# The value columns of a gated block: two column groups by a seven-product scheme, and twelve gate dot products moved to the last stage

## The chip, the cores and the metric

The kernel runs on one core of one Trainium2 chip. TensorE (PE) multiplies matrices, VectorE (DVE) and ScalarE (ACT) work on elements, GpSimd (POOL) and SyncE (SP) here mostly issue transfers, which all share the core's 16 DMA engines. The metric is the device time of one execution in microseconds; lower is better.

## The reference, cut to what matters

One layer on 512 tokens of width 2048, all in float32:

```python
shift, scale, gate = split(silu(c) @ W_ada + b_ada, 3)
h = rmsnorm(x) * (1 + scale) + shift
q_lat, kv_lat, k_rope, z_mla, u, v, z_sgu, g_mla, g_sgu = split(h @ W_in)
A = attention(q_lat, kv_lat, k_rope) * silu(z_mla)           # 16 heads, causal
B = u * (tril(W_s) @ rmsnorm(v) + b_s) * silu(z_sgu)         # 16 column groups, chunks of 128 tokens
x = x + gate * ((sigmoid(g_mla) * A + sigmoid(g_sgu) * B) @ W_out)
return rmsnorm(x)
```

The change touches how the 2048 columns of v are computed (`h @ W_in[:, v]`, a product of 512 x 2048 by 2048 x 2048) and when the 2048 values of `gate` are (each a dot product of silu(c) with one column of W_ada).

## The kernel before, in words

**Precision.** Each float32 operand is split in a high part (`hi`, a cast to the fast float32 format by ScalarE) and a low part (`lo = x - hi`, by VectorE). A product is three matmuls: hi hi, lo hi, hi lo (`mm3`). A tile of 128 x 1024 weights is a granule; class `Stream` (`ws`) loads granules in order on SP's queue into three buffers (`wraw0..2`) and splits them into two places of parts (`w0`, `w1`), one granule ahead of the matmuls.

**Stages.** (1) Two streams `w1`, `w2` give the latents; meanwhile VectorE takes the dot products of W_ada for scale and shift (`ada_dot`, one 128 x 2048 tile each, 16 values per 128 columns and part) and the input is scaled in place (`fix_to`) into `hh[j]` (high) and `hl[j]` (low), 16 chunks of 128 inputs by 512 tokens. (2) The columns of v with those of k_rope, in five column groups of widths `VW`, tokens on the partitions: for each of 8 granules, 2 chunks and 4 blocks of 128 tokens one `mm3` into four banks (line 518). At the end of a group `evac_v` takes the sum of squares and copies the bank out, and the copy is stored to `v_d`. Beside them VectorE runs the 16 dots for `gate` (`gate_step`), scales the latents (`lat_scale`), and makes sums and differences of quarters of the input (`make_sums`, `split_sum`, tiles s1, s2, s3, s4). Then one plain column group (z of head 14) runs, 4 slots from -4 to -1. (3) The main stage: columns of z, g, u, s, t in pairs. Each pair takes seven products of 1024 inputs by 256 tokens by 128 columns instead of eight (Strassen's scheme, Winograd's form): the right sides are the quarters of the input and s1 to s4, the left ones quarters of the weights and their sums, made by VectorE (`add`) or by accumulating transfers of GpSimd. A slot is one product, 24 matmuls of 256 tokens (lines 1267 to 1269).

**The order around the change** is written out beforehand. `on(s, phase, f)` puts work at slot s in a phase (FIRST, EVAC, GATE, SPLIT, BACK, then after the matmuls MISC, LOAD); `place(s, us, f)` seeks the first slot from s on in which VectorE's planned time stays under 2.75 us (`spend` books it). A product's weights are split two slots ahead, into three places w0, w2, w1. Every engine works its queue in order. Functions in `early` run at a step of stage 2; those in `pend` are taken one at a time as granules are fetched; `stores` issues a store one step after its copy. (4) Attention, head by head. (5) The output product: four column groups of 512 with 8 granules each (`out_granule`), `residual` after each, which multiplies with `grow`, the gate broadcast to all partitions, read from `gate_row` in memory. `gate_to_row` (line 877) transposes the gate on TensorE and writes that row in slot 10 of the main stage. The granules of the fourth group are split early into tiles of their own (`last_tiles`).

Of the kernel before, what the change touches and what calls it, by code (L numbers as in the profile page):

```python
# [11 lines left out]
F32 = mybir.dt.float32  # L12
# [8 lines left out]
P = 128  # L21
D = 2048
S = 512
# [13 lines left out]
VW = (512, 512, 384, 384, 320)  # L37
# [3 lines left out]
DOTS = (3, 3, 4, 5, 5, 6, 7, 8, 9, 9, 10, 11, 11, 12, 12, 13, 13, 14, 14, 15, 16, 16, 16, 16)  # L41
FIXED = (0, 0, 0, 0, 2, 2, 2, 2, 2, 4, 4, 4, 6, 6, 8, 8, 10, 10, 12, 12, 14, 16, 16, 16)
# [73 lines left out]
def trunk_layer(ctx, tc, xT, xn, c, vecs, pos, wada, w1, w2, wv, wv3, wv4, wh, wh15, wq, wqr, wk, wvv, wo, wsT, bsp, gfin, out,  # L116
# [91 lines left out]
    gate_row = scratch("gate_row", [KC, P])  # L208
    v_d = scratch("v_d", [NB, P, D])
# [42 lines left out]
    def last_tiles():  # L252
        k = len(dlast)
        dlast.append((nt(dp[0].p, [P, GW], F32R, f"dh{k}"), nt(dp[0].p, [P, GW], F32R, f"dl{k}")))
        return dlast[-1]

    go = {}
# [238 lines left out]
    for n, i in enumerate((8, 0, 9, 12, 1, 10, 11, 2, 7, 3, 4, 5, 6)):  # L496
        early.setdefault(8 + n, []).append(lambda i=i: lat_scale(i))
# [4 lines left out]
    for j in range(8):  # L502
        at_ = 12 + 5 * j // 2
        early.setdefault(at_, []).append(lambda j=j, at_=at_: sums_begin(j, at_))
        early.setdefault(32 + j, []).append(lambda j=j: split_sum("s4", j, s4f[j]))
    for cg, w in enumerate(VW):
        psv = [bank()[:, :w] for _ in range(4)]
        for i in range(8):
            g = cg * 8 + i
            wH, wL = get(gv[g], ahead=1)  # L510
            if g < 8:
                fix_to(FIXED[KC + g], lambda: dot_to(DOTS[KC + g]))
            for k in range(2):
                j = 2 * i + k
                sl = slice(k * w, (k + 1) * w)
                for n in range(NB):
                    tk = slice(n * P, (n + 1) * P)
                    mm3(psv[n], hh[j][:, tk], hl[j][:, tk], wH[:, sl], wL[:, sl], j == 0, j == KC - 1)
            for j in gate_step.get(g, ()):
                ada_dot(2 * KC + j)  # L520
            if g == 31:
                ada.close()
                c1[0] = Scope("c1", side=RIGHT)
                for n in ("s4h", "s4l"):
                    sums[n] = nt(c1[0].p, [P, 8, 256], F32R, n)
            for f in early.pop(g, ()):
                f()
            stores()
        if cg == 0:
# [4 lines left out]
            tb = Scope("tB")  # L534

        def evac_v(n, cg, ps):
            m = VW[cg] // P
            w, c0 = m * P, sum(VW[:cg])
            junk = nt(tb.p, [P, S], F32, f"t{n % 2}") if cg == 0 else nt(latp.p, [P, S], F32, f"lat{10 + n % 2}")
            ACT.activation(junk[:, :w], ps[:, :w], AF.Square, accum_out=ssv[:, n, cg:cg + 1])  # L540
            t = nt(tb.p, [P, S], F32, "sig", bufs=2)
            ACT.copy(t[:, :VW[cg]], ps[:, :VW[cg]])
            store(v_d[n][:, c0:c0 + w], t[:, :w])
            if cg == 4:
                store(kr_d[n], t[:, w:VW[cg]])

        for n in range(NB):
            pend.append(lambda n=n, cg=cg, ps=psv[n]: evac_v(n, cg, ps))
# [6 lines left out]
    pend.append(v_norm)  # L555
# [1106 lines left out]
```

## Time and profile before

| | |
|---|---|
| median of 3 runs | 1610.45 us (1609.62 to 1610.47) |
| profiled execution | 1609.98 us, its span 1608.3 us |
| PE / DVE / ACT busy | 99% / 72% / 47% of the span |
| two 512-wide groups of v | 154.31 to 241.35 us |
| two 384-wide groups, one of 320 | 241.35 to 309.17 to 337.32 us |
| plain column group | 337.32 to 348.23 us |
| main stage | from 348.23 us |
| output product | from about 1422 us, between the last head's work |

The page gives busy time by engine, forty slices of the span with granted clock and DMA load, the DMA queues, the chain of work that ended last, the costliest groups of instructions and the DMA issues. In a row of a group stand line, engine, operation, tiles out<-in, shape, count, busy time, mean ns of one, and the idle time before it with what ended it. Matmuls are pipelined, so a matmul's own duration is longer than its distance from the next.

### The profile page before, as it was taken

Reading aid. Unit: us, or ns where it says so; the run is one execution under the profiler, and the core shown is the slowest. Engines: PE = TensorE matmul, PEld = TensorE weight load, DVE = VectorE, ACT = ScalarE, POOL = GpSimd, SP = SyncE. Lnnn points to the kernel's source line nnn. Section 1 sums busy time; section 2 is a strip of 40 time slices with the busy share of each in tenths; the row PEclk is TensorE's granted clock in tenths of the full one; section 3 lists DMA queues with packets and bytes.
Section 4 is the critical chain, followed back from the end, with each engine's and each line's share of the span. In section 5 each row is a group of like instructions: output and inputs, shape, how many; then the busy total and the mean of one; then the engine's idle time right before and its main releaser. Section 6 shows DMA issues by size and latency. Waiting matters only on the chain.

```text
span 1608.3 us, 26988 instructions
## 1 busy us (share of the span) xinstructions
PE 1594.2 (99%) x10760; PEld 1488.5 (93%) x10760; DVE 1165.3 (72%) x1719; ACT 755.5 (47%) x1259; POOL 105.4 (7%) x128
## 2 busy tenths in 40 slices
PE   9999999999999999999999999999999999999997
PEld 8888889999999999999999999999988889888886
DVE  8989679658777777777677777666777888763453
ACT  4443334355545454454465554554655554542322
POOL 0000000001111111111111111112000000000000
PEclk9999999999999999999999999999999999999999
DMA  9988489568899897898887998887422233336422
GB/s 379 354 296 317 171 280 324 170 193 202 219 253 252 226 252 214 233 258 212 231 253 203 250 268 207 238 193 181 162 87 88 82 105 89 90 109 227 136 87 105
DMA packets 122766, 329.64 MB, mean 205 GB/s; under 512 B 14072, under 2 KB 35600, under 8 KB 115856
## 3 DMA queue, kind: packets, MB, share of 16 engines
q1 hardware_dynamic: 104768, 269.72, 48.0%
q0 software_dynamic: 17872, 58.20, 20.8%
q8 instruction: 84, 1.38, 0.3%
q14 instruction: 42, 0.34, 0.1%
HBM read 303.95 MB, written 23.93 MB: 204 GB/s over the span
## 4 chain that ended last, share of the span: by engine, by line
PE 90%; DVE 4%; DMA 2%; ACT 1%; issue 1%; SPq 0%; DVEq 0%; ACTq 0%
PE ps L1267 15%; PE ps L1269 15%; PE ps L1268 15%; PE ps L136 14%; PE ps L137 14%; PE ps L135 14%; PE ps L1429 1%; DVE wada L126 1%; PE ps L1392 1%; PE ps L1393 1%; DVE t L123 1%; DMA wraw<-in_w 1%; DMA lat<-v_d 1%; DVE lat L123 1%; DMA rope_d<-half 0%
## 5 line engine op out<-in xcount | busy, mean ns | idle before, releaser
L106 DVE TENSOR_TENSOR w0l<-wraw,w0h 128x1024 fp32r<-128x1024 f32 (+3 forms) x74 | 78.8, 1066 | 58.8 <-ACT w0h L105 58.5
L105 ACT CAST w1h<-wraw 128x1024 fp32r<-128x1024 f32 (+3 forms) x74 | 63.9, 863 | 118.8 <-PE ps L137 57.7
L1267 PE MATMUL ps<-hh,w0h 128*128 128x256 f32 x416 | 118.5, 285 | 0.9 <-DVE lat L123 0.9
L105 ACT CAST w0h<-wraw 128x1024 fp32r<-128x1024 f32 (+3 forms) x74 | 68.9, 931 | 106.6 <-PE ps L137 66.5
L1269 PE MATMUL ps<-hh,w0l 128*128 128x256 f32 x416 | 117.7, 283 | 0.0
L1268 PE MATMUL ps<-hl,w0h 128*128 128x256 f32 x416 | 117.7, 283 | 0.0
L106 DVE TENSOR_TENSOR w1l<-wraw,w1h 128x1024 fp32r<-128x1024 f32 (+3 forms) x74 | 73.1, 988 | 59.6 <-ACT w1h L105 58.6
L1267 PE MATMUL ps<-hh,w2h 128*128 128x256 f32 x400 | 113.5, 284 | 0.0
L1267 PE MATMUL ps<-hh,w1h 128*128 128x256 f32 x400 | 113.4, 283 | 0.0
L1268 PE MATMUL ps<-hl,w1h 128*128 128x256 f32 x400 | 113.2, 283 | 0.0
L1269 PE MATMUL ps<-hh,w2l 128*128 128x256 f32 x400 | 113.2, 283 | 0.0
L1268 PE MATMUL ps<-hl,w2h 128*128 128x256 f32 x400 | 113.2, 283 | 0.0
L1269 PE MATMUL ps<-hh,w1l 128*128 128x256 f32 x400 | 113.2, 283 | 0.0
L126 DVE SCALAR_TENSOR_TENSOR wada<-wada,cact 128x2048 f32<-128x2048 f32 x47 | 107.1, 2280 | 0.0
L123 DVE TENSOR_TENSOR w2l<-raw,w2h 128x1024 fp32r<-128x1024 f32 x56 | 68.5, 1224 | 39.0 <-ACT w2h L649 38.9
L136 PE MATMUL ps<-w0l,hh 128*128 128x256 f32 (+3 forms) x288 | 92.7, 322 | 0.1
L135 PE MATMUL ps<-w0h,hh 128*128 128x256 f32 (+3 forms) x288 | 92.7, 322 | 0.0
L137 PE MATMUL ps<-w0h,hl 128*128 128x256 f32 (+3 forms) x288 | 92.4, 321 | 0.0
L135 PE MATMUL ps<-hh,w1h 128*128 128x512 f32 x226 | 89.7, 397 | 0.0
L136 PE MATMUL ps<-hl,w1h 128*128 128x512 f32 x226 | 88.3, 391 | 0.8 <-DVE hl L126 0.8
L137 PE MATMUL ps<-hh,w1l 128*128 128x512 f32 x226 | 88.1, 390 | 0.0
L629 POOL DMA_DIRECT2D wraw<-in_wh x67 | 59.2, 939 | 439.8 <-DVE w0l L123 211.7
(350 smaller groups left out, 5400.5 us busy)
## 6 DMA issues: line engine op xcount, KB each, us to landing
raw<-in_wh SPq DMA_DIRECT2D x105, 512.0 KB, 6.9
wada<-in_wada SPq DMA_DIRECT2D x47, 1024.0 KB, 7.4
wraw<-in_wh POOLq DMA_DIRECT2D x67, 512.0 KB, 6.9
wraw<-in_wh SPq DMA_DIRECT2D x45, 512.0 KB, 7.8
raw<-in_wh POOLq DMA_DIRECT2D x42, 512.0 KB, 7.8
wraw<-in_wo SPq DMA_DIRECT2D x32, 512.0 KB, 3.7
half<-in_w SPq DMA_DIRECT2D x35, 256.0 KB, 5.4
wraw<-in_w SPq DMA_DIRECT2D x16, 512.0 KB, 8.9
```

Source lines behind the costliest of these rows:

```text
L105: self.nc.scalar.copy(hi[:, :n], raw[:, :n])
L106: self.nc.vector.tensor_tensor(out=lo[:, :n], in0=raw[:, :n], in1=hi[:, :n].bitcast(F32), op=ALU.subtract)
L123: DVE.tensor_tensor(out=out, in0=in0, in1=in1, op=op)
L126: DVE.scalar_tensor_tensor(out=out, in0=in0, scalar=scalar, in1=in1, op0=op0, op1=op1, **kw)
L135: PE.matmul(ps, ah, bh, start=start, stop=False)
L136: PE.matmul(ps, ah, bl, start=False, stop=False)
L137: PE.matmul(ps, al, bh, start=False, stop=stop)
L629: q_.dma_start(t, wh[h, n, q // 10 - 1], **eng)
L1267: PE.matmul(ps, wH[:, sl], xh, start=st, stop=False, skip_group_check=True)
L1268: PE.matmul(ps, wH[:, sl], xl, start=False, stop=False, skip_group_check=True)
L1269: PE.matmul(ps, wL[:, sl], xh, start=False, stop=sp, skip_group_check=True)
L1392: PE.matmul(ps, q2[:, q], krh[:, :n], start=False, stop=False)
```

## The change: what it does

- Columns 0 to 1023 of v, two groups of 512 before, are computed together by the seven-product scheme: quarters of the input are 1024 inputs by 256 tokens, quarters of the weights 1024 inputs by 512 columns. `V7` lists 28 steps (product, granule of two chunks), placed at slots -28 to -1; a step has 2 chunks x 2 token blocks x 3 matmuls with the tokens as the stationary operand and 512 columns moving. The sums of the weights are made by VectorE (`v_sum`, `v_t3`) and, for product 4, by accumulating transfers of GpSimd. The results are combined from banks y, z, w by `v_copy`, `v_c12`, `v_c22`, `v_c11`, `v_c21`.
- The three narrower groups come first (26 steps with the plain column group's two granules among them), then the seven products, then the main stage. The plain columns go to memory (`z_d`) and are loaded back.
- Of the 16 dots for the gate four stay in stage 2 (`NG`); twelve (`chunk_load`, `chunk_sum`) go to the output product, one per granule. For them silu(c) is stored (`cact_d`) and broadcast back. The gate is written to `gate_row` in four parts straight from its column form (`gate_out`), and read in four parts (`grow_load`); the transpose goes. The tiles for the fourth group lie in two scopes of their own.
- The main stage's first loads are placed at slots -7 to -2; the sums s1 to s4 are made some steps earlier; v's norm (`v_norm`) moves to slot 1.

```diff
-VW = (512, 512, 384, 384, 320)
+VW = (384, 384, 320)
+VC = (1024, 1408, 1792)
+
+V7 = [(p, i) for i in range(4) for p in (1, 6)] + [(p, i) for i in range(4) for p in (2, 7)]
+V7 += [(3, i) for i in range(4)] + [(p, i) for i in range(4) for p in (5, 4)]
+NG = 4
 WARM = (32, 48)
 CR = 8
 
-DOTS = (3, 3, 4, 5, 5, 6, 7, 8, 9, 9, 10, 11, 11, 12, 12, 13, 13, 14, 14, 15, 16, 16, 16, 16)
-FIXED = (0, 0, 0, 0, 2, 2, 2, 2, 2, 4, 4, 4, 6, 6, 8, 8, 10, 10, 12, 12, 14, 16, 16, 16)
+DOTS = (3, 3, 4, 5, 5, 6, 7, 8, 9, 9, 10, 11, 11, 12, 12, 13, 13, 14, 14, 15, 16, 16, 16, 16, 16)
+FIXED = (0, 0, 0, 0, 2, 2, 2, 2, 2, 4, 4, 4, 6, 6, 8, 8, 10, 10, 12, 12, 14, 14, 16, 16, 16)
...
-    gv = [ws.add(src[i], 2 * w) for w, src in zip(VW, (wv[0], wv[1], wv3[0], wv3[1], wv4)) for i in range(8)]
     gq, gr, gk, gvv = {}, {}, {}, {}
     c1 = [None]
-    gz = [ws.add(wh[H - 2, 0, half], GW) for half in range(2)]
-    ws.limit = gz[1]
+
+    def third_place():
+        return [nt(c1[0].p, [P, GW], F32R, tag) for tag in ("w2h", "w2l")]
+
+
+    steps = [("z", 0)] + [(0, i) for i in range(8)] + [("z", 1)] + [(cg, i) for cg in (1, 2) for i in range(8)]
+    gb = []
+    for cg, i in steps:
+        if cg == "z":
+            gb.append(ws.add(wh[H - 2, 0, i], GW))
+        else:
+            last = (cg, i) == (2, 7)
+            gb.append(ws.add((wv3[0], wv3[1], wv4)[cg][i], 2 * VW[cg], to=third_place if last else None))
+    ws.limit = gb[-1]
...
-    gate_step = {}
-    for j in range(KC):
-        st = 8 + (3 * j) // 2
-        gate_step.setdefault(st, []).append(j)
-        load_before(gv[0] + st + 1 if st < 31 else gv[0] + 31, ada_load, 2 * KC + j)
+    for j in range(NG):
+        load_before(gb[8 + j], ada_load, 2 * KC + j)
+    load_before(g2[0], lambda: DMA.dma_start(cact_d, cact[0:1]))
...
+    kept_at = [(lambda: c1[0].p, "raw7")] + [(lambda: wp, f"wraw{i}") for i in (1, 2, 0)]
+    kept, passing, vparts = {}, {}, {}
+
+    def v_kept(i):
+        p, tag = kept_at[i]
+        kept[i] = nt(p(), [P, GW], F32, tag)
+        DMA.dma_start(kept[i], wv[1][i])
+
+    def v_pass(what, i):
+
+        n = len(passing)
+        t = passing[what, i] = nt(c1[0].p, [P, GW], F32, ("raw6", "raw4", "raw5")[n % 3])
+        g, half = {"11": (0, 0), "11b": (0, 0), "21": (0, 4), "22": (1, 4)}[what]
+        DMA.dma_start(t, wv[g][half + i])
+
+    def v_sum(what, i):
+        tt(kept[i], kept[i], passing[what, i], ALU.add)
+
+    def v_t3(i):
+        t = passing["11b", i]
+        tt(t, kept[i], t, ALU.subtract)
+
+    def v_split(g):
+        p, i = V7[g]
+        t = kept[i] if p in (6, 2, 4) else passing[{1: "11", 7: "22", 3: "11b", 5: "21"}[p], i]
+        pl, tag = [(wp, "w1"), (wp, "w0"), (c1[0].p, "w2")][g % 3]
+        vparts[g] = hi, lo = nt(pl, [P, GW], F32R, tag + "h"), nt(pl, [P, GW], F32R, tag + "l")
+        hilo(hi, lo, t)
+
+    for at_, f, *a in ((20, v_pass, "11", 0), (21, v_kept, 0), (22, v_pass, "11", 1), (23, v_kept, 1), (24, v_kept, 2),
+                       (24, v_pass, "11", 2), (24, v_split, 0), (25, v_kept, 3), (25, v_sum, "11", 0), (25, v_split, 1),
+                       (25, v_pass, "11", 3)):
+        early.setdefault(at_, []).append(lambda f=f, a=a: f(*a))
+
+    plain = bank()
+    v_banks = [(4, 5, 6, 7), (0, 1, 2, 4), (5, 6, 7, 3)]
+    ring_ = [6, 7, 0, 1, 2]
+    assert (n_bank[0] - 1) % 8 == 3
+    psv = {}
...
+    def gate_sum(a, b):
+
+        cols = slice(a, b)
+        tt(gate[:, cols], dots[:, 2 * KC + a:2 * KC + b], vec[:, C_BADA + 2 * KC + a:C_BADA + 2 * KC + b], ALU.add)
+
+    def gate_out(a, b):
+        DMA.dma_start(gate_row[a:b].rearrange("j p -> p j"), gate[:, a:b])
 
     def v_norm():
-        tt(gate, dots[:, 2 * KC:], vec[:, C_BADA + 2 * KC:C_BADA + 3 * KC], ALU.add)
+        gate_sum(0, NG)
...
+    V = -len(V7)
+    for g in range(len(V7)):
+        spend(V + g - 2, 1.22)
+    v_events = [(V - 2 + 2 * i, GATE, v_sum, "11", i) for i in range(1, 4)]
+    v_events += [(V + 5 + 2 * i, GATE, v_sum, "22", i) for i in range(4)]
+    v_events += [(V + s, GATE, v_t3, i) for i, s in enumerate((13, 14, 16, 17))]
+    for s, *_ in v_events:
+        spend(s, 1.22)
+    v_events += [(V + g - 2, SPLIT, v_split, g) for g in range(2, len(V7))]
+    for what, slots in (("22", (1, 3, 5, 8)), ("11b", (10, 12, 14, 15)), ("21", (16, 17, 18, 19))):
+        v_events += [(V + s, LOAD, v_pass, what, i) for i, s in enumerate(slots)]
+    v_events += [(V + 15 + i, LOAD, lambda i: nc.gpsimd.dma_start(kept[i], wv[0][4 + i], accum_op=ALU.add), i)
+                 for i in range(4)]
+    for s, ph, f, *a in v_events:
+        on(s, ph, f, *a)
     for j in range(8):
-        place(-2 + j // 4, 0.42, lambda j=j: hilo(hh[j][:, right], hl[j][:, right], s3f[j]))
+        assert place(V + 1, 0.42, lambda j=j: split_sum("s4", j, s4f[j])) < V + 8 + j // 2
+    for j in range(8):
+        assert place(V + 6, 0.42, lambda j=j: hilo(hh[j][:, right], hl[j][:, right], s3f[j])) < V + 15 + j // 2
+    v7 = {}
+
+    def v_copy(name, ps, tags):
+        for t in range(2):
+            v7[name, t] = slot(tags[t]) if tags[t][:3] == "lat" else nt(tb.p, [P, S], F32, tags[t])
+            ACT.copy(v7[name, t], v7[ps][t])
+
+    def v_done(s, n, part, c0, t, src=None):
+
+        ACT.activation(slot("lat12") if src is None else t, src or t, AF.Square, accum_out=ssv[:, n, part:part + 1])
+        if src is not None:
+            ACT.copy(t, src)
+        on(s + 1, LOAD, lambda: DMA.dma_start(v_d[n][:, c0:c0 + 512], t))
+
+    def v_c12(s):
+        for t in range(2):
+            o = v7["u2", t]
+            tt(o, v7["z"][t], o, ALU.subtract)
+            v_done(s, t, 3, 512, o)
+
+    def v_c22(s):
+        for t in range(2):
+            o = v7["z6", t]
+            tt(o, o, v7["y"][t], ALU.subtract)
+            v_done(s, 2 + t, 3, 512, o)
+
+    def v_c11(s):
+        for t in range(2):
+            o = v7["p1", t]
+            tt(o, v7["w"][t], o, ALU.add)
+            v_done(s, t, 4, 0, o)
+
+    def v_c21(s):
+        for t in range(2):
+            v_done(s, 2 + t, 4, 0, slot(("lat7", "lat9")[t]), v7["y"][t])
+
+    on(V + 7, EVAC, v_copy, "p1", "y", ("lat11", "lat4"))
+    on(V + 8, EVAC, v_copy, "z6", "z", ("lat5", "lat6"))
+    on(V + 15, EVAC, v_copy, "u2", "y", ("t0", "t1"))
+    on(V + 18, EVAC, v_c12, V + 18)
+    on(V + 20, EVAC, v_c22, V + 20)
+    on(V + 27, EVAC, v_c11, V + 27)
+    on(0, EVAC, v_c21, 0)
+    on(1, EVAC, v_norm)
+    on(2, LOAD, gate_out, 0, NG)
+    for s in (18, 20, 27):
+        spend(V + s, 1.38)
...
-    def gate_to_row():
-        pg = bank()
-        PE.transpose(pg[:KC, :P], gate, ident)
-        row = sig()[:KC, :P]
-        DVE.tensor_copy(row, pg[:KC, :P])
-        DMA.dma_start(gate_row, row)
-
-    on(10, MISC, gate_to_row)
...
+    for g, (p, i) in enumerate(V7):
+        s = done[0] = V + g
+        for f in pend[:1]:
             f()
-        del pend[:2]
+        del pend[:1]
+        for f in early.pop(len(steps) + g, ()):
+            f()
         if s == -1:
-            while pend:
-                pend.pop(0)()
+            assert not pend and not early
             tb.close()
             mis = Scope("more")
             sg[0] = Scope("sgu")
-        run(s, FIRST, EVAC, GATE)
-        if s == -4:
-            plain = bank_at(plain_bank)
-        for k in range(4):
-            j = (s + 4) * 4 + k
-            sl = slice(j % 8 * P, (j % 8 + 1) * P)
-            mm3(plain, wH[:, sl], wL[:, sl], hh[j], hl[j], j == 0, j == KC - 1)
-        run(s, SPLIT, BACK, MISC, LOAD)
+        run(s, FIRST, EVAC, GATE, SPLIT, BACK)
+        if i == 0 and p in (1, 5, 6):
+            which, banks = {1: ("y", (2, 4)), 6: ("z", (0, 1)), 5: ("w", (5, 6))}[p]
+            v7[which] = [bank_at(k) for k in banks]
+        ps = v7["y" if p < 5 else "z" if p > 5 else "w"]
+        wH, wL = vparts.pop(g)
+        for k in range(2):
+            xh, xl = rights[p](2 * i + k)
+            sl = slice(k * 512, (k + 1) * 512)
+            st, sp = i == k == 0 and p in (1, 5, 6), i == 3 and k == 1
+            for t in range(2):
+                tk = slice(t * P, (t + 1) * P)
+                PE.matmul(ps[t], xh[:, tk], wH[:, sl], start=st, stop=False, skip_group_check=True)
+                PE.matmul(ps[t], xl[:, tk], wH[:, sl], start=False, stop=False, skip_group_check=True)
+                PE.matmul(ps[t], xh[:, tk], wL[:, sl], start=False, stop=sp, skip_group_check=True)
+        run(s, MISC, LOAD)
...
+    last_of[0] = Scope("last", side=RIGHT)
+    da = Scope("ada2")
+    cact = nt(da.p, [P, D], F32, "cact")
+    DMA.dma_start(cact, bcast(cact_d, D))
+    chunks, later = {}, {}
+
+    def grow_load(cg):
+        cols = slice(cg * S, (cg + 1) * S)
+        DMA.dma_start(grow[:, cols], bass.AP(tensor=gate_row.tensor, offset=gate_row.offset + cg * S, ap=[[0, P], [1, S]]))
+
+    def chunk_load(j):
+        chunks[j] = nt(da.p, [P, D], F32, "wada", bufs=2)
+        DMA.dma_start(chunks[j], wada[2 * KC + j])
+
+    def chunk_sum(j):
+        t = chunks.pop(j)
+        stt(t, t, 1.0, cact, ALU.mult, ALU.mult, accum_out=dots[:, 2 * KC + j:2 * KC + j + 1])
+        if j % 4 == 3:
+            gate_sum(j - 3, j + 1)
+
+
+    chunk_at = dict(zip(range(NG, KC), (2, 3, 4, 5, 6, 8, 9, 10, 11, 12, 13, 14)))
+    for j, st in chunk_at.items():
+        later.setdefault(st, []).append(lambda j=j: chunk_sum(j))
+        later.setdefault(st if j + 2 < KC else 99, []).append(lambda j=j: chunk_load(j + 2))
+        if j % 4 == 3:
+            later.setdefault(st + 1, []).append(lambda j=j: gate_out(j - 3, j + 1))
+            later.setdefault(st + 2, []).append(lambda j=j: grow_load(j // 4))
+    later.pop(99)
+    for j in (NG, NG + 1):
+        chunk_load(j)
+
+    def no_more_chunks():
+        da.close()
+        last_of[1] = Scope("last1", side=RIGHT)
+
+    later[chunk_at[KC - 1]].append(no_more_chunks)
+    load_before(go[0, 7], lambda: (grow_load(0), DMA.dma_start(gfb, bcast(gfin, D))))
```

More of the change, by code (lines that the diff above doesn't have):

```diff
@@ L502, in trunk_layer, with evac_v @@
     for j in range(8):
-        at_ = 12 + 5 * j // 2
+        at_ = 11 + 2 * j
         early.setdefault(at_, []).append(lambda j=j, at_=at_: sums_begin(j, at_))
[L505 to L512, printed above, removed]
+    def evac_v(n, cg, ps):
+        m = VW[cg] // P
+        w, c0 = m * P, VC[cg]
+        t = nt(tb.p, [P, S], F32, "sig", bufs=2)
+        ACT.activation(t[:, :w], ps[:, :w], AF.Square, accum_out=ssv[:, n, cg:cg + 1])
+        ACT.copy(t[:, :VW[cg]], ps[:, :VW[cg]])
+        store(v_d[n][:, c0:c0 + w], t[:, :w])
+        if cg == 2:
+            store(kr_d[n], t[:, w:VW[cg]])
@@ L678, in trunk_layer @@
             if k == 0:
-                load(k, q)
+                on({11: -7, 12: -5, 22: -3, 21: -2}[q], LOAD, load, k, q)
             else:
```

98 lines of the change are left out of this document (55 added, 43 removed).

## The prediction

> **What bounds the kernel now.** I read the page's first two parts, its chain, then a table by stage that I cut where the width of the matmuls changes.
>
> ```profile
> span 1608.3 us, 26988 instructions
> PE 1594.2 (99%) x10760; PEld 1488.5 (93%) x10760; DVE 1165.3 (72%) x1719; ACT 755.5 (47%) x1259; POOL 105.4 (7%) x128
> ...
> PEclk9999999999999999999999999999999999999999
> ...
> PE 90%; DVE 4%; DMA 2%; ACT 1%; issue 1%; SPq 0%; DVEq 0%; ACTq 0%
> ```
>
> TensorE is busy throughout, at full clock, and holds 90% of the chain. A busy share counts overlapped matmuls, so the count per stage says more. Columns: time, then busy (count) of PE, PEld, DVE, ACT, POOL, then clock, DMA share, GB/s.
>
> ```profile
> 154.31:241.35 87.04, 87.04 (x386) 72.07 (x385) 61.38 (x76) 30.67 (x45) 0.00 (x0) 1.00 0.68 232
> 241.35:309.17 67.82, 67.55 (x385) 66.43 (x384) 61.18 (x94) 25.48 (x52) 0.00 (x0) 1.00 0.77 268
> 309.17:337.32 28.15, 28.15 (x193) 28.15 (x193) 10.05 (x16) 12.20 (x28) 0.00 (x0) 1.00 0.63 190
> ...
> 348.23:390.00 41.77, 40.45 (x335) 40.02 (x334) 30.94 (x53) 23.89 (x43) 4.07 (x6) 1.00 0.70 174
> 390.00:433.00 43.00, 42.50 (x353) 42.09 (x352) 32.33 (x57) 25.47 (x43) 4.97 (x7) 1.00 0.87 232
> 433.00:470.00 37.00, 37.00 (x310) 37.00 (x310) 28.66 (x37) 15.99 (x21) 5.13 (x6) 1.00 0.91 242
> ...
> 1432.00:1500.00 68.00, 68.00 (x311) 56.62 (x309) 28.92 (x34) 18.56 (x26) 0.00 (x0) 1.00 0.51 185
> 1500.00:1588.00 88.00, 88.00 (x390) 72.88 (x389) 43.08 (x59) 27.94 (x42) 0.00 (x0) 1.00 0.34 113
> 1588.00:1608.30 20.30, 11.84 (x98) 11.60 (x96) 6.88 (x17) 4.18 (x11) 0.00 (x0) 0.89 0.29 103
> ```
>
> The first row is the two 512-wide column groups of v: 2 x 192 matmuls (the counts take in the neighbours at the edges) in 87.04 us, 0.227 us each, with no stall. The second is the two 384-wide groups. There the weight loads are busy 66.43 of 67.82 us, so 1.4 us are stalls; VectorE, at 61.18, makes the sums of the input and 16 gate dot products beside them. The first two rows of the main stage need 0.1194 us a matmul by the steady row (37.00 / 310): 41.77 - 335 x 0.1194 = 1.8 and 43.00 - 353 x 0.1194 = 0.8, so 2.6 us of stalls.
>
> **The change part by part.**
>
> *Matmuls.* Seven products over 256 tokens, 1024 inputs and 512 columns: 7 x 4 granules x 2 chunks x 2 token blocks x 3 = 336 of width 512, against 384. 48 x 0.227 = 10.9 us less on the path; the operands keep their roles (tokens stationary, 512 columns moving), so the price holds. The transpose of the gate (one matmul) goes too: nothing counted.
>
> *The 384-wide groups* now hold four gate dots instead of most of sixteen. Durations:
>
> ```profile
> L126 DVE SCALAR_TENSOR_TENSOR wada<-wada,cact 128x2048 f32<-128x2048 f32 x20 | 45.7, 2284 | 0.0
> L106 DVE TENSOR_TENSOR w1l<-wraw,w1h 128x1024 fp32r<-128x1024 f32 x9 | 11.0, 1225 | 15.3 <-ACT w1h L105 15.3
> L123 DVE TENSOR_TENSOR t<-hh,hl 128x512 f32<-128x512 f32 x16 | 10.3, 684 | 0.0
> ...
> L106 DVE TENSOR_TENSOR w0l<-wraw,w0h 128x768 fp32r<-128x768 f32 x8 | 7.6, 952 | 4.1 <-ACT w0h L105 4.1
> ...
> L123 DVE TENSOR_TENSOR t<-t,t 128x256 f32<-128x256 f32 x16 | 6.7, 421 | 0.3
> ...
> L106 DVE TENSOR_TENSOR w1l<-wraw,w1h 128x640 fp32r<-128x640 f32 x4 | 3.3, 826 | 7.7 <-ACT w1h L105 7.7
> ...
> L123 DVE TENSOR_TENSOR raw<-raw,raw 128x1024 f32<-128x1024 f32 x2 | 2.4, 1216 | 0.0
> ```
>
> One make_sums is 2 x 0.68 + 4 x 0.42 = 3.05, its s1 and s2 splits 0.84, so with two low parts (1.90) and two lat_scale (1.37) a pair of steps asks 7.2 us of VectorE, against 2 x 24 x 0.173 = 8.3 of TensorE (66.43 / 384 = 0.173). The stalls go: -1.4 (ends -2.5 and 0). Next late there is nothing on VectorE; the weights' transfers have three buffers ahead.
>
> *Entry to the seven products.* A step has 12 matmuls, 2.72 us. Summed from the second-last 320-wide step to product step 11: VectorE has 0.83 + 0.84 + 1.22, then 3.05 + 1.22 + 1.22, then per step a split (1.22) and a sum (1.22) or three small splits (1.26): 38.8 us in all, against 2 x 24 x 0.1466 + 12 x 2.72 = 39.7 of TensorE (28.15 / 192 = 0.1466). There is no room at the start. Followed in order: make_sums(7) ends 3.5 us into the last 320-wide step, v_sum 4.7, ScalarE's cast (1.05) 5.8, the low part 7.1; TensorE wants it at 3.5 + 2.7 + 0.45 = 6.7: 0.4 lost. The next split waits behind split_sum(7) and a v_sum: 0.6 lost. Two evacuations later ScalarE waits for a store that SP holds behind a v_pass load, which itself waits for a split: 0.6. I take +1.7. Ends: 0 (all covered) and +6: VectorE's densest row is 61.18 of 67.82, 90%; at that density 38.8 us take 43.0, +3.5, and the waits between cast and low part may add as much again.
>
> *Loads of the products.* Before: 16 x 512 KB. Now 24, four by POOL with accumulation.
>
> ```profile
> q1 hardware_dynamic: 104768, 269.72, 48.0%
> q0 software_dynamic: 17872, 58.20, 20.8%
> ```
>
> From the DMA view of the main stage's start (KB each, median us from issue to landing):
>
> ```profile
> raw<-in_wh SPq DMA_DIRECT2D x12, 512.0 KB, 8.5
> wraw<-in_wh POOLq DMA_DIRECT2D x7, 512.0 KB, 7.0
> ```
>
> At a full share, 512 KB cost 1.5 us plain (269.72 MB in 772 us) and 3.0 accumulated (58.20 MB in 335). In product steps 14 to 20 six plain and four accumulated ones ask 21 us in 16.3, a backlog of 5. The tightest, "11b" 2 and 3, have 11.6 us from the freeing of their place to use, of which sum, cast and low part take 3.5, so 8.1 are left to land in; "21" 0 has 12.4 less 2.4. The 8.5 us of the row above would miss the first by 0.4, a transfer on quieter queues (3.7, in the last stage's rows below) would not: 0 (ends 0 and +3). Behind a late one stand v_t3, VectorE's next splits, and SP's stores of v. The plain column's 256 KB now go out and come back, with some twenty steps between: nothing.
>
> *Joint with the main stage.* ScalarE's rows:
>
> ```profile
> L105 ACT CAST w1h<-wraw 128x1024 fp32r<-128x1024 f32 x9 | 9.5, 1053 | 24.9 <-PE ps L137 15.0 <-issue 9.9
> ...
> L730 ACT ACTIVATE lat<-lat 128x512 f32<-128x512 f32 x6 | 3.8, 630 | 1.0 <-DVE lat L123 1.0
> ...
> L542 ACT COPY sig<-ps 128x512 f32<-128x512 f32 x8 | 4.7, 582 | 7.1 <-DMA v_d<-sig 7.1
> ...
> L730 ACT ACT_TABLE_LOAD x2 | 2.6, 1283 | 0.0
> ...
> L540 ACT ACTIVATE t<-ps 128x512 f32<-128x512 f32 x4 | 2.4, 590 | 0.0
> ```
>
> In slot 0 (2.86 us) ScalarE gets v_c21, 2 x (0.59 + 0.19 + 0.58) = 2.7, the sigmoid of z 14 with its table 1.9, then the cast 1.05; in slot 1 the square root of v_norm with a table of its own, 1.6, and a second sigmoid table after it. The low part for slot 2 then ends 1.9 us late. Against that the main stage's loads come earlier and the plain column's copy leaves the joint; of the old 2.6 I leave 1.3. 3.2 - 2.6 = +0.6 (ends -2.6 and +3).
>
> *Last stage.* Twelve dots, 27.4 us of VectorE, in 13 granules (5.44 us each), where it has 28.92 of 68 us busy: beside a split and a residual (three 0.68) a granule asks 5.6, and 6.8 in the first two of the third column group (two splits each), made up in the next two. The transfers are the question: cact, twelve 1 MB chunks and the gate's parts join the weights, x and the final gain on SP, and each chunk load waits for the dot two before it; a dot whose chunk is late holds VectorE and so the next split.
>
> ```profile
> DMA  5052050700064100199999997963240506060423
> GB/s 195 7 110 100 0 185 31 202 11 0 0 210 157 52 0 0 8 352 406 390 433 423 408 408 234 403 161 156 52 164 7 203 0 197 13 172 38 88 121 44
> ...
> wraw<-in_wo SPq DMA_DIRECT2D x17, 512.0 KB, 3.7
> ```
>
> ```profile
> 1441.55 0.42 SPq L1535 DMA_DIRECT2D gbc<-gate_row  x1
> ```
>
> ```profile
> 1458.90 1.23 DVE L106 TENSOR_TENSOR w0l<-wraw,w0h 128x1024 fp32r<-128x1024 f32 x1 [4.22 <-ACT w0h L105]
> ```
>
> The chunk buffers lie where head 15's tiles were, so loads start at 1441.5, where SP turns to the gate's row now. The split at 1458.90 is that of granule 7's weights, begun with granule 6 at 1457.6; those weights come behind 4.25 MB and land at about 1456, in time. Queued up to chunk 8: 13.75 MB (14.4e6 bytes). The rows above give DMA share and GB/s in forty slices of 2.5 us from 1400. At the 400 GB/s of the full ones it lands at 1441.5 + 36 + about 2 = 1479.5, and VectorE is ready for it at 1479.6. Its dot (2.28) and a split (1.22) end at 1483.1; TensorE wants that split at 1457.6 + 5 x 5.44 = 1484.8. +0.5 (ends 0 and +3). The Trainium skill, "DMA: Bandwidth & Descriptors", Specifications, gives 358 GB/s as a core's share of HBM; by that chunk 8 would land at 1484 and the sum would be 2 us higher. The trace's slices of 403 to 433 GB/s go against it. The gate's quarters, written in 4-byte pieces, have some eight granules until used; they cost SP's queue only.
>
> Sum against the profiled execution's own 1609.98 us (span 1608.3; the median shown is 0.47 higher): 1609.98 - 10.9 - 1.4 + 1.7 + 0.6 + 0.5 = 1600.5.
>
> **The rivals.**
>
> *VectorE becomes the bound of the products.* For it: 38.8 of 39.7 us. Against it: later steps hold one split and less. Entry +3.5 instead of 1.7 and the joint at +3 instead of 0.6: 1604.7.
>
> *No new stall shows.* The first main rows show what a two-step lead can absorb: entry 0, joint -1.3, last stage 0: 1609.98 - 10.9 - 1.4 - 1.3 = 1596.4. Against it: the entry's order above.
>
> *Slower: the copies crowd the last stage.* It decides below about 280 GB/s: chunk 8 then lands at 1495, 13.7 us after the last moment that costs nothing (1484.8 less dot and split), and TensorE stands behind VectorE: 1613.7; at 250 GB/s 1501 and 1620. Also the case in which the change does not do what it says, the dots being moved only to be waited for. Against it: seven slices of 352 to 433 at that very place.
>
> *The clock falls.* The last row of the stage table has a mean of 0.89: in the tail without matmuls the clock drops. A pause of over 4 us would do it, costing itself and some 2 us more: two such, 1612. The Trainium skill, "TensorE: Matmul & The Clock Gate", Part 1, puts the half clock after about 3.4 us idle. The trace agrees in the tail only; the longest pauses that I expect are under 2 us.
>
> **How the numbers follow.** Forecast 0.62; VectorE bound 0.18; no new stall 0.11; last stage crowded 0.06; clock 0.03. About 0.2% (3.2 us) is what a measurement can tell here from no change. The first three cases are faster but for a tenth of VectorE's and a little of the forecast's tail: 0.87; same 0.06; slower 0.07. The ends added together give 1594 and 1611; for 8 in 10 the range goes from below "no new stall", 1595.5, past VectorE's case, 1606.5.
>
> **What would show it.** Right: 336 matmuls of width 512 in about 78 us between the 320-wide group and the main stage; pauses of TensorE under 1 us in its first four steps, released by VectorE's low parts; one of about 2 us at slot 2, behind ScalarE; the last stage's matmuls still at 0.227. Wrong: matmuls of the products spaced over 0.24 on the mean, with waits on "passing" loads; VectorE idle behind wada in the last stage; a clock below 1.00 before the tail.

## The result, and the profile after

| | |
|---|---|
| before, same chip | 1610.16 us |
| after | 1629.78 us (1628.35 to 1633.24) |
| ratio | 1.0125, 95% interval 1.0108 to 1.0143: slower |
| forecast | 1600.5 us (1595.5 to 1606.5) |
| spans, before and after | 1608.3 and 1626.6 us, 18.3 us longer |

The page of the changed kernel, the lines that answer to those shown of before:

```profile
span 1626.6 us, 27010 instructions
PE 1594.7 (98%) x10711; PEld 1484.2 (91%) x10711; DVE 1197.8 (74%) x1751; ACT 770.2 (47%) x1273; POOL 107.9 (7%) x132
...
PEclk9999999999999999999999999999999999999899
...
PE 83%; DMA 7%; DVE 5%; ACT 2%; issue 2%; SPq 0%; DVEq 0%; ACTq 0%
```

There are 49 matmuls fewer, as planned. But DMA now holds 7% of the chain instead of 2%, and the clock row, flat before, has an 8 near its end. A busy share of 98% hides where; a cut by stage shows it. The columns are: time, PE busy (count), granted clock, DMA share, GB/s. First before: the 384- and 320-wide groups, the plain column group, the start of the main stage, and the last stage (from the last transpose of attention to the last matmul). Then after: the same groups with a plain granule of 5.5 us between them, the seven products, the start of the main stage, the last stage.

```profile
241.35:337.18 95.83, 95.56 (x577) 1.00 0.73 245
337.18:348.23 11.05, 11.05 (x51) 1.00 0.63 195
348.23:433.00 84.77, 82.95 (x686) 1.00 0.79 203
1433.80:1599.56 165.76, 165.76 (x782) 1.00 0.40 140
```

```profile
160.60:266.70 106.10, 103.30 (x600) 0.98 0.59 199
266.70:347.06 80.36, 77.87 (x339) 1.00 0.63 182
347.06:432.00 84.94, 81.83 (x668) 0.98 0.86 208
1435.22:1617.32 182.10, 172.63 (x782) 0.96 0.63 202
```

Read the second number against the first (idle time) and then the clock.

- The last stage has the same 782 matmuls and takes 16.3 us more: 9.5 us idle, and 6.9 us by which the same matmuls take longer. 13.7 us ran at half clock (below); TensorE was busy in 9.6 of them, so the clock explains some 4.8 of the 6.9.
- The groups take 106.1 us. By the rows of before they should take 384 x 0.173 + 192 x 0.1466 + 5.5 = 100.1.
- The products take 80.4 us; 336 x 0.227 + 1.7 = 77.9 was forecast.
- So the main stage starts at 347.06 instead of 348.23: of some 10.6 us that v should have given, 1.2 are left, and the last stage loses 16.3.

**The last stage.** First the forty slices of 1 us from 1480 to 1520 of the DMA view (busy tenths, GB/s), then the same stretch's rows for what holds the next weights (chain that ended last: start, length, what).

```profile
DMA  9999999989998614998699999999989899938685
GB/s 381 414 418 451 381 353 144 140 33 33 33 33 33 33 16 131 426 397 336 203 440 451 426 381 430 451 418 389 291 369 401 311 369 378 197 57 123 74 147 102
```

```profile
1509.06 10.73 DMA gate_row<-gate
1519.81 0.33 SPq L1685
...
1520.71 8.36 DMA wraw<-in_wo
...
1529.17 1.05 ACT w1h L110
```

The gate's quarter of 2 KB, 512 pieces of 4 bytes, is issued near 1481. From the seventh slice on the rate falls from 353 GB/s and more to 144 and then to 33, with the engines still counted busy (tenths of 8 and 9, and a 6 in the last of the slices at 33): they count as busy and move next to nothing. The second quarter goes out at 1509.06 and takes 10.73 us to land. SP, which must read it back (line 1685), stands there until 1519.81, and the weights' loads stand behind it in SP's queue; the next load is issued at 1520.71, takes 8.36 us, and ScalarE's cast starts at 1529.17. TensorE's clock there:

```profile
1525.00:1527.10 2.10, 0.10 (x1) 0.99 0.98 414
1527.10:1537.34 10.24, 6.61 (x15) 0.50 0.49 193
...
1554.40:1557.82 3.42, 2.96 (x7) 0.51 0.76 261
```

**The 384-wide groups.** The chain, one row of ScalarE's timeline (in brackets the wait before it), then windows with all engines (PE, PEld, DVE, ACT, POOL, clock, DMA share, GB/s):

```profile
201.59 3.42 DMA v_d<-sig
205.03 0.59 ACT sig L528 x2
...
207.02 0.85 ACT w0h L110
...
213.53 0.84 ACT w1h L110
```

```profile
213.05 0.58 ACT L536 COPY sig<-ps 128x512 f32<-128x512 f32 x1 [5.20 <-DMA v_d<-sig]
```

```profile
207.00:214.00 7.00, 5.62 (x30) 4.72 (x28) 4.29 (x8) 1.80 (x4) 0.00 (x0) 1.00 0.55 187
214.00:216.30 2.30, 1.32 (x6) 1.07 (x7) 1.90 (x4) 1.71 (x4) 0.00 (x0) 1.00 0.02 5
216.30:219.72 3.42, 3.42 (x13) 3.42 (x12) 3.42 (x7) 0.00 (x0) 0.00 (x0) 0.51 1.03 293
```

ScalarE copies the banks out through the staging tile `sig`, which has two buffers; a store must free one before the next copy. In two steps running it takes two banks each of the group before, and in the step after them the plain columns' bank (line 536). Twice it waits for a store, at 205.03 and at 213.05; its cast of the weights stands behind the copy, and TensorE waits for the cast: 1.4 + 1.0 us of pauses, and then 3.4 us at half clock. VectorE, which I had costed step by step here, is not in it.

### The profile page after: what moved, and what is told of

The parts are those of the page before. It is cut to its first block, busy times and chain, and to the rows that moved or that the text cites. A ratio compares the mean times of both kernels' runs of the same rounds, so it can differ in the third digit from the quotient of the medians.

```text
span 1626.6 us, 27010 instructions
## 1 busy us (share of the span) xinstructions
PE 1594.7 (98%) x10711; PEld 1484.2 (91%) x10711; DVE 1197.8 (74%) x1751; ACT 770.2 (47%) x1273; POOL 107.9 (7%) x132
## 4 chain that ended last, share of the span: by engine, by line
PE 83%; DMA 7%; DVE 5%; ACT 2%; issue 2%; SPq 0%; DVEq 0%; ACTq 0%
PE ps L1409 15%; PE ps L1411 15%; PE ps L1410 14%; PE ps L141 11%; PE ps L142 11%; PE ps L140 11%; DMA wada<-in_wada 1%; PE ps L1571 1%; DMA wraw<-in_wo 1%; PE ps L1390 1%; PE ps L1389 1%; PE ps L1388 1%; DVE wada L131 1%; DMA wraw<-in_wh 1%; DMA gate_row<-gate 1%
## 5 line engine op out<-in xcount | busy, mean ns | idle before, releaser
L128 DVE TENSOR_TENSOR w2l<-raw,w2h 128x1024 fp32r<-128x1024 f32 x62 | 75.9, 1224 | 44.7 <-ACT w2h L726 39.0
L110 ACT CAST w1h<-wraw 128x1024 fp32r<-128x1024 f32 (+3 forms) x65 | 54.6, 841 | 100.5 <-PE ps L142 40.3
L110 ACT CAST w0h<-wraw 128x1024 fp32r<-128x1024 f32 (+3 forms) x66 | 60.4, 915 | 78.4 <-issue 26.4
L111 DVE TENSOR_TENSOR w0l<-wraw,w0h 128x1024 fp32r<-128x1024 f32 (+3 forms) x66 | 69.2, 1048 | 34.2 <-ACT w0h L110 33.9
L111 DVE TENSOR_TENSOR w1l<-wraw,w1h 128x1024 fp32r<-128x1024 f32 (+3 forms) x65 | 62.5, 962 | 34.0 <-ACT w1h L110 33.0
L128 DVE TENSOR_TENSOR w1l<-wraw,w1h 128x1024 fp32r<-128x1024 f32 x46 | 56.3, 1224 | 41.9 <-ACT w1h L726 37.9
L128 DVE TENSOR_TENSOR w0l<-raw,w0h 128x1024 fp32r<-128x1024 f32 x52 | 63.6, 1223 | 31.9 <-ACT w0h L726 23.9
L128 DVE TENSOR_TENSOR w0l<-wraw,w0h 128x1024 fp32r<-128x1024 f32 x46 | 56.3, 1224 | 38.9 <-ACT w0h L726 37.1
```

Of the source, the lines that this page charges most:

```text
L110: self.nc.scalar.copy(hi[:, :n], raw[:, :n])
L111: self.nc.vector.tensor_tensor(out=lo[:, :n], in0=raw[:, :n], in1=hi[:, :n].bitcast(F32), op=ALU.subtract)
L128: DVE.tensor_tensor(out=out, in0=in0, in1=in1, op=op)
```

## The experiments

**1. Rows instead of pieces.** The late quarters are transposed on TensorE and written as four rows of 512 bytes:

```diff
+    def gate_rows(a, b):
+        pg = bank_at(4 if a == 12 else 0)
+        PE.transpose(pg[:4, :P], gate[:, a:b], ident)
+        DVE.tensor_copy(rows[:4], pg[:4, :P])
+        DMA.dma_start(gate_row[a:b], rows[:4])
...
-            later.setdefault(st + 1, []).append(lambda j=j: gate_out(j - 3, j + 1))
+            later.setdefault(st + 1, []).append(lambda j=j: gate_rows(j - 3, j + 1))
```

> Edit: the three late quarters of the gate are transposed on TensorE (one small transpose each), copied by VectorE and written as four rows of 512 bytes; chunk loads, dots and reads back stay. Theory 'pieces' (a 2 KB write in 512 pieces of 4 bytes holds all 16 DMA engines for about 9 us, and the weights behind it come late): the last stage, 1434 to 1617 (183 us) in the changed kernel, falls to 167 to 169, the time to 1613 to 1616. Rival 'crowd' (the 1 MB chunks are too much beside the weights, whatever the gate's write looks like): 1626 or more. Rival 'queue' (SP stands still until the gate's write has landed, and that alone makes the weights late): as 'pieces', since a write in rows lands in about 3 us.

Measured 1618.6 us, ratio 1.0048 (1.0031 to 1.0065): 11.2 us less than the change, and 2.6 above the range of 'pieces'. The last stage (PE alone) has no half clock left:

```profile
1437.27:1608.97 171.70, 168.32 (x785) 1.00 0.58 214
```

That is 10.4 us less than the 182.10 of the change, and 5.9 more than before. The pieces hold for most of the last stage's loss, not for all of it and not for all of the kernel's.

**2. The pieces on another queue.** Writes and reads back of the late quarters are issued by GpSimd, so that SP does not stand still:

```diff
+            later.setdefault(st + 1, []).append(lambda j=j: gate_out(j - 3, j + 1, nc.gpsimd))
+            later.setdefault(st + 2, []).append(lambda j=j: grow_load(j // 4, nc.gpsimd))
```

> Edit: the three late gate writes, still in 4-byte pieces, and the three reads back are issued by GpSimd's queue, so that SP never waits for them. 'Pieces': the engines stand still all the same, 1623 to 1630. 'Queue': 1613 to 1616. 'Crowd': 1628 to 1630.

Measured 1633.1 us, ratio 1.0142 (1.0127 to 1.0157): no gain, and above every range that was expected. SP's queue is not the cause: the loss is no smaller when SP neither issues the late pieces nor waits for them. Why it is 3 us larger is not shown.

**3. The pieces without the chunks.** The twelve late dots are left out, with their 1 MB loads and the broadcast of silu(c), so the late gate holds its bias alone; the writes in pieces stay:

```diff
-    DMA.dma_start(cact, bcast(cact_d, D))
...
-        chunks[j] = nt(da.p, [P, D], F32, "wada", bufs=2)
-        DMA.dma_start(chunks[j], wada[2 * KC + j])
+        chunks[j] = None
...
-        stt(t, t, 1.0, cact, ALU.mult, ALU.mult, accum_out=dots[:, 2 * KC + j:2 * KC + j + 1])
+        DVE.memset(dots[:, 2 * KC + j:2 * KC + j + 1], 0.0)
```

> The twelve late dots are left out, with their chunk loads and the broadcast of silu(c); the gate there is the bias alone. Writes in 4-byte pieces and reads back stay, on SP. 'Crowd': the last stage is back at 167, 1612 to 1614. 'Pieces' and 'queue': the freezes stay; the three weight buffers cover the first two, the third, in the column group with two granules of weights a step, still costs: 1616 to 1624.

Measured 1623.4 us, ratio 1.0084 (1.0069 to 1.0099). With 12 MB of copies gone, the chain still reads

```profile
1537.23 10.35 DMA wraw<-in_wo
```

so the pieces hold up the weights without any chunk beside them. The chunks and their dots are worth 6.4 us here, the difference to the change. My rival "the copies crowd the last stage" falls as the main cause.

**4. The front repaired, the pieces kept.** One evacuation a step in the 384-wide groups, stores ahead of loads in the steps of the products, the sigmoid of the plain columns in slot 4 of the main stage instead of slot 0:

```diff
-        wH, wL = get(gb[st], ahead=0 if st == len(steps) - 1 else 1, run={0: 3, 9: 2, 10: 2}.get(st, 1))
+        wH, wL = get(gb[st], ahead=0 if st == len(steps) - 1 else 1, run={0: 3}.get(st, 1))
...
+        stores()
         run(s, MISC, LOAD)
-        stores()
...
-    gate_op("z", 14, gate_src[0], 0)
+    gate_op("z", 14, gate_src[0], 4)
```

> Last stage untouched; three edits ahead of it: one evacuation of the first 384-wide group a step instead of two (then ScalarE should not wait for a staging tile's store), the stores of a product step issued ahead of its loads, and the sigmoid of z 14 four slots later. Theory 'staging' (the stalls of the 384-wide groups, 5.2 us with a stretch at half clock, and 2.8 us at the entry of the products come from ScalarE waiting for stores that come late on SP): the 384-wide groups take 66.5 to 67.5 us instead of 71.7, the entry loses under 1.2 us, the start of the main stage 1 us or less instead of 3.1: 1619 to 1622. Rival 'VectorE is the bound' (it has 38.8 us of work in 39.7): the groups gain, the entry's 2.8 us stay: 1622 to 1625.

Measured 1625.1 us, ratio 1.0089 (1.0072 to 1.0106), above the 1619 to 1622 of 'staging'. Groups, products, and the start of the main stage:

```profile
159.49:260.54 101.05, 100.61 (x600) 1.00 0.63 209
260.54:338.99 78.45, 77.27 (x340) 1.00 0.65 186
338.99:423.76 84.77, 79.88 (x657) 1.00 0.85 205
```

The groups win back 5.0 us of the 6.0 they had lost, the products 1.9 of 2.5. The waits for the staging tile's stores, not VectorE, were the cause. But the third row has 4.9 us idle, where 1 or less was expected: the first quarter of the gate is written in pieces too, at slot 2 (issued at 348.9). The DMA slices of 1 us from 340 to 380 show the hole again: from the sixteenth on seven slices of 12 to 94 GB/s, most with the engines counted busy, and a load of v behind it. (The low slices before them, from the seventh on, are idle engines.)

```profile
DMA  9779970009889992979675999999999889710098
GB/s 268 49 131 223 285 301 2 16 33 291 303 324 129 193 258 12 53 41 53 53 70 94 193 229 262 291 271 243 213 293 340 186 343 410 299 41 4 0 119 147
```

```profile
359.47 13.37 DMA lat<-v_d
```

**5. Everything repaired ('best').** Experiments 1 and 4 together, and the first quarter transposed and written in slot 10:

```diff
-    on(2, LOAD, gate_out, 0, NG)
+    on(10, MISC, first_rows)
```

> As 'rows', and besides one evacuation a step in the 384-wide groups, the stores before the loads in the steps of the products, the sigmoid's first part ten granules earlier, and the gate's first quarter transposed on TensorE and written as four rows of 512 bytes in granule 10, so that no 4-byte piece is left in the kernel. If the four losses found so far (last stage, staging tile, entry to the products, first quarter) are separate and add up, the time is that of 'rows' (1618.6) less 3.6 for the groups, 1.9 for the entry, 2 to 3 for the start of the main stage: 1609 to 1612, no more than 2 us from the kernel before. If they hide one another (a pause that goes makes the next one longer), 1614 to 1619. If the pieces of the first quarter are what holds the main stage's start, no pause over 1.5 us stands between 345 and 375 us of the span.

Measured 1606.54 us, ratio 0.9978 (0.9969 to 0.9988): faster than before.

```profile
160.09:261.33 101.24, 100.63 (x601) 1.00 0.64 208
261.33:339.71 78.38, 77.34 (x339) 1.00 0.65 186
339.71:424.48 84.77, 83.70 (x693) 1.00 0.82 212
1424.44:1595.11 170.67, 168.27 (x786) 1.00 0.58 216
```

It is 12.1 us better than 'rows', more than the 7.5 to 8.5 that the expectation's terms add up to (its range, 1609 to 1612, allows 6.6 to 9.6): in 'rows' the first 84.5 us of the main stage held 5.5 us idle, here 1.1. Most of what I had put down to ScalarE's order at the joint hung on the first quarter's pieces. The clock is full from end to end of the four stages.

**6. The chunks earlier ('spread').**

```diff
-    chunk_at = dict(zip(range(NG, KC), (2, 3, 4, 5, 6, 8, 9, 10, 11, 12, 13, 14)))
+    chunk_at = dict(zip(range(NG, KC), (2, 3, 4, 5, 6, 7, 8, 9, 10, 11, 12, 13)))
```

> As 'best', with the last seven chunks of the gate's weights loaded and summed one granule earlier each, so that the last stands in granule 13 instead of 14. If what is left in the last stage is the chunks' sums crowding VectorE at its end, 1 to 2 us less than 'best'. If it is the share of the DMA engines that the chunks' 12 x 0.5 MB take from the weights, the same as 'best' within 1 us, the pauses in other granules.

Measured 1605.06 us (1604.89 to 1605.18), ratio 0.9966 (0.9954 to 0.9979): the best of the versions that do the whole work, 5 us under before. The intervals of 'best' and 'spread' overlap. (A chunk has 1 MB, not the 0.5 of the expectation.) In the profile the stretch from 1500 to 1525, with 2.4 us idle in 'best', has none here, and 0.8 appear in 1475 to 1500:

```profile
1475.00:1500.00 25.00, 24.19 (x105) 1.00 0.83 299
1500.00:1525.00 25.00, 25.00 (x112) 1.00 0.74 250
```

**7. The seven products without the late dots ('products').** 'best' with the twelve dots left out by the edit of experiment 3; the late gate holds its bias alone.

> As 'best', with the twelve late dot products of the gate left out (no chunk loads, no sums; the late gate holds its bias alone): the seven-product part by itself. The matmuls saved (10.9) less the entry (about 1.7 to 2.8) and a joint of 1 to 3 us put it at 1600 to 1604 if the seven products are worth what I forecast and the dots cost what is left; at 1608 to 1612 if the products themselves bring next to nothing even without the other losses.

Measured 1601.42 us, ratio 0.9944 (0.9931 to 0.9958). Products and last stage:

```profile
261.22:339.58 78.36, 77.29 (x340) 1.00 0.64 187
...
1424.71:1591.84 167.13, 167.13 (x786) 1.00 0.42 139
```

**8. The other part alone ('dots_only').** The kernel before, v's groups untouched, with the twelve dots late and the pieces:

```diff
+NG = 4
...
-    on(10, MISC, gate_to_row)
+    on(2, LOAD, gate_out, 0, NG)
...
+            later.setdefault(st + 1, []).append(lambda j=j: gate_out(j - 3, j + 1))
+            later.setdefault(st + 2, []).append(lambda j=j: grow_load(j // 4))
```

> The kernel before with the second part of the change alone: twelve of the dot products for the gate in the last stage, and the gate written in 4-byte pieces as in the change; v's column groups as they were. If the loss is the pieces' and independent of the seven products, the last stage is 14 to 17 us longer than before and the 384-wide groups 1 to 2 us shorter or, by the staging tile, up to 4 longer: 1622 to 1630. If the last stage suffers only together with the seven products' other timing, it stays under 1615.

Measured 1632.9 us, ratio 1.0141 (1.0125 to 1.0156), a little above my range: this part alone loses more than the whole change.

```profile
241.03:335.62 94.59, 94.59 (x576) 1.00 0.52 155
...
1434.94:1621.62 186.68, 175.37 (x782) 0.95 0.65 197
```

The first row shows its whole gain, 95.83 - 94.59 = 1.2 us in the 384-wide groups (forecast 1.4). The second shows its price, 20.9 us.

**9. What about a piece of 4 bytes is dear?** Four kernels, each 'best' with one extra write of each late quarter that nobody reads or waits for. They differ in where the bytes land, 'sixteen' also in the size and number of its pieces; each kernel has one of the four lines, and the comments are added here:

```diff
+    apart = scratch("apart", [4, P, P])          # 512 pieces of 4 bytes, 512 bytes apart
+    sixtyfour = scratch("sixtyfour", [4, P, 16]) # 512 pieces of 4 bytes, 64 bytes apart
+    near = scratch("near", [P, 4])               # "sixteen": 128 pieces of 16 bytes, side by side
+    beside = scratch("beside", [4, P])           # 512 pieces of 4 bytes, side by side
...
+ DMA.dma_start(apart[:, :, 0].rearrange("j p -> p j"), gate[:, j - 3:j + 1])
```

> As 'best' (all four quarters of the gate transposed and written as rows), with one more write of each late quarter beside it, into a scratch that nobody reads: 512 pieces of 4 bytes that lie 512 bytes apart in DRAM, where the change's 512 pieces lay next to one another. If the 4-byte piece itself is the price, the engines stand as before: rates near 30 GB/s for some 9 us behind each of the three writes, last stage 11 to 16 us longer than 'best', 1617 to 1623. If it is that many pieces fall into the same few hundred bytes, the writes cost little: below 1609, no stretch of the DMA row under 100 GB/s behind them.

> As 'best', with one more write of each late quarter into a scratch that nobody reads: 128 pieces of 16 bytes, side by side (the same 2 KB in a quarter of the pieces). If the price is per piece, a quarter of the freeze: some 2 us behind each write, 1607 to 1611. If it is per byte or per write, the whole 9 us again and 1617 to 1623; if it is for pieces of 4 bytes alone, the time of 'best' (1606.5) within 1.5 us.

> As 'apart', with the extra 512 pieces of 4 bytes written side by side into a 2 KB scratch that nobody reads, the one difference being where they land. If neighbouring pieces are the price, the freeze is back: some 9 us near 30 GB/s behind each of the three writes and 1614 to 1624. If it was the reading back of the pieces, or that the rest of the kernel waits for them, that made the change slow, the time of 'apart' (1606.1) within 1.5 us.

> As 'apart', with the extra pieces 64 bytes apart instead of 512. If only pieces in the same 64 bytes hold one another up, the time of 'apart' (1606.1) within 1.5 us; if pieces in the same 512 bytes do, an eighth as many share a block as in 'beside', and the write lands in 5 to 10 us instead of 2 to 5: 1607 to 1614.

| | time us | ratio | one write lands in (min/median/max us) |
|---|---|---|---|
| 512 x 4 bytes, 512 apart | 1606.1 | 0.9978 (0.9968 to 0.9987) | 1.8/3.3/4.8 |
| 512 x 4 bytes, 64 apart | 1606.1 | 0.9977 (0.9968 to 0.9987) | 1.8/3.2/4.6 |
| 128 x 16 bytes, side by side | 1606.8 | 0.9981 (0.9972 to 0.9991) | 1.9/3.4/4.9 |
| 512 x 4 bytes, side by side | 1623.6 | 1.0082 (1.0067 to 1.0097) | 9.9/10.0/10.0 |

Two windows, the 12.5 us behind the first write and a later stretch, of 'apart' and then of 'beside' (all engines, clock, DMA share, GB/s):

```profile
1472.50:1485.00 12.50, 12.42 (x55) 9.97 (x54) 10.60 (x12) 3.36 (x7) 0.00 (x0) 1.00 0.82 273
1500.00:1525.00 25.00, 22.46 (x97) 17.70 (x96) 20.49 (x24) 7.06 (x11) 0.00 (x0) 1.00 0.69 226
```

```profile
1472.50:1485.00 12.50, 12.50 (x56) 10.10 (x55) 10.60 (x13) 3.33 (x6) 0.00 (x0) 1.00 1.02 111
1500.00:1525.00 25.00, 18.48 (x75) 14.58 (x74) 15.40 (x17) 5.83 (x9) 0.00 (x0) 0.87 0.89 242
```

Same bytes, same number of pieces, same queue, no reader: in 'beside' the engines are busy throughout (1.02) and move 111 GB/s, in 'apart' 273 at a lower share. That costs 17.1 us against 'best', and shows the cause: 512 pieces of 4 bytes next to one another in DRAM. My expectation that the price is the piece itself fell with 'apart', and "a quarter of the freeze" with 'sixteen'. The Trainium skill, "DMA: Bandwidth & Descriptors", Specifications, says that a transfer below 512 B turns into a read-modify-write. That would fit pieces which share a block and must wait for one another, but by size alone it does not give the result: three of the four extra writes have pieces far below 512 B too and cost at most 0.2 us. Nor is a shared 512-byte stretch enough: at 64 bytes apart eight pieces share one, and nothing is lost. What happens inside the memory stays open, and so does whether 8-byte pieces, fewer than 512 neighbours, or another order of the pieces, would pass.

## Why the prediction was wrong

The span forecast was 1608.3 - 9.5 = 1598.8; it came out at 1626.6, 27.8 us above. By the steps of the prediction:

- *Matmuls*, -10.9: right. 48 matmuls fewer, at 0.227 each; with everything else repaired the products take 78.4 us, 2.2 above 336 x 0.227.
- *Last stage*, +0.5: **the step that failed**, 15.8 of the 27.8 us. "The gate's quarters, written in 4-byte pieces, have some eight granules until used; they cost SP's queue only." They do not: three writes of 2 KB hold all transfers, weights included, down to means of 63, 131 and 48 GB/s for 10, 8 and 9 us (1486 to 1496, 1514 to 1522 and 1542 to 1551 us). Written in rows the late quarters give back 10.4 of the stage's 16.3 us (experiment 1); experiments 3 and 9 show that neither the chunks nor the reading back is needed for the loss. I costed the write by its bytes and by when its reader needs it, never by what it does to the transfers beside it; no row of before had such a write (the row was transposed there), and I gave this no bounds from both sides.
- My rival for "slower" had the right sign and the wrong cause. Rates below 280 GB/s did come, but from the pieces. The rate that the forecast took, 400 GB/s, holds ahead of the first hole (the first five slices shown, 381 to 451), and chunk 8, on which the +0.5 was worked out, was there when its dot began at 1483.06. The chunks have a price nevertheless: the dots cost 1605.06 - 1601.42 = 3.6 us in 'spread' and 5.1 in 'best', against 0.5 forecast, with ends of 0 and +3.
- *384-wide groups*, -1.4: VectorE's relief came as forecast (-1.2 in 'dots_only'), but the step looked at VectorE alone. Two evacuations in one step behind one staging tile, on ScalarE, cost 5.0 us (experiment 4); in all the groups came out 6.0 above the forecast. The prediction counts the waits for a store at the entry alone.
- *Entry to the products*, +1.7: the wait that I named ("ScalarE waits for a store that SP holds behind a v_pass load") is the one in the chain, but longer: the store took 3.66 us and held the cast to 277.77. The products took 4.2 us above their matmuls; with the store ahead of the load 2.2 to 2.3. VectorE was not the bound: that rival falls. (Its work as listed adds up to at most 38.1 us, not 38.8; it changes nothing.)

```profile
272.34 0.33 SPq L554
...
273.20 3.66 DMA kr_d<-sig
...
277.77 1.06 ACT w0h L145
```

- *Joint*, +0.6: the 3.0 us wait behind ScalarE was there as described (the wait view's row below), but from the main stage's start to the last stage the kernel loses some 2.6 us more than before.

```profile
PE ps L1409 <- ACT lat L835: 3.0, 1, 3.0
```

- *Clock*: "A pause of over 4 us would do it" was wrong. 1.4 and 1.0 us of pauses inside 9 us were followed by 3.4 us at half clock (the last section has what decides it). In all some 20 us ran at half clock (3.4 + 3.4 + 10.2 + 3.4). TensorE was busy in 16.4 of them, so they cost some 8 us, nearly half of what the change lost against before.
- *Range*: its ends were added wrongly. With the loads' +3 the upper one is 1614, not 1611; the measured 1629.8 lies above both.

## What to carry to other kernels

Never write a tile's columns to neighbouring 4-byte words of DRAM beside a stream of loads: transpose first and write rows, or place the words 64 bytes apart; the price is paid by every other transfer, not by the write alone. When a part is moved next to another engine's work, follow the staging tiles and stores behind the evacuations as closely as the arithmetic. Two changes packed in one should be costed and run apart: here the seven products were worth 8.6 us ('products' against before on the same chip) and the late dots cost 3.6 to 23, for 1.2 us gained. ('products' leaves the twelve dots out altogether, so its 8.6 us hold what VectorE saves by that.) Seven products with all dots left in place would by these numbers be the better kernel, if VectorE has room for them there; that was not tried.

## What the hardware showed that I had not expected

- 512 pieces of 4 bytes side by side: 33 GB/s for six slices of 1 us while the engines count as busy (tenths of 6 to 9), and 10 us to land; the same pieces 64 bytes apart: a median of 3.2 us and nothing lost.
- Half clock after short pauses, and inside the kernel always in steps of about 3.4 us. The Trainium skill, "TensorE: Matmul & The Clock Gate", "What's actually happening", has the half clock come after an idle window of about 3.4 us. The steps agree (3.42 us in the rows above), the threshold does not: no pause in the 9 us before 216.30 was longer than 1.4 us, and the 7.6 us before those had none. A longer sum of pauses (2.4 us of 25 in 'best') passed at full clock, so a sum over a long stretch does not decide it either. What does decide it, the traces show: the idle time in one window of a fixed grid.

In each of the fourteen traces all changes of the clock lie whole multiples of 3.413 us apart. Cut by that grid, every one of the 31 half clocks (the ends of the kernels included) follows a window in which TensorE was idle for 1.684 us or more, about half of it. None of the other windows at full clock, some 6500, had more than 1.677. So a pause of one length can go both ways, by where it falls. The wait of slot 2 behind ScalarE did: 2.95 us in the change, from 352.98, and 2.96 in 'rows', from 353.37. In the change it lies in one window, and the next is at half clock; in 'rows' an edge of the grid cuts it in two, and the clock stays full. First the change, then 'rows' (time, PE busy, clock, DMA share, GB/s):

```profile
352.87:356.28 3.41, 0.46 (x4) 1.00 0.40 147
356.28:359.70 3.42, 3.42 (x19) 0.50 0.26 30
```

```profile
351.41:354.82 3.41, 1.96 (x17) 1.00 0.89 247
354.82:358.23 3.41, 1.90 (x16) 1.00 0.03 5
358.23:361.64 3.41, 3.41 (x31) 1.00 0.56 186
```
